# Row maxima of the next attention window: from five separate places of the loop to the two blocks of value products, with seven PSUM banks in one ring

## The chip, the cores and the metric

One core of one Trainium2 chip runs the whole kernel in one launch. The metric is the device time of one execution in microseconds; the figure for a kernel is the median of its runs. Views of the profile come from one further, profiled execution of the same program. The engines are called by the profile's short names: PE (TensorE, the matmuls), PEld (its weight loads), DVE (VectorE), ACT (ScalarE), POOL (GpSimd), SP (SyncE, which issues most DMAs).

## The reference, cut to what matters

The kernel computes one transformer layer with two mixers side by side: a convolution branch and a grouped-query attention branch fed by one input projection, merged by gates, then one output projection.

```python
# x (1, 1024, 1024), ctx (1, 256, 1024); 16 query heads of 64, 4 key/value heads
h  = rms_norm(x, g_pre) * (1 + sc) + sh          # hc the same from ctx
ua, gate_a, q, k, v, gate_b, gm = split_proj(h @ w_in)
q = apply_rope(rms_norm(q, q_norm_g));  k = apply_rope(rms_norm(k, k_norm_g))
k_all, v_all = latent and context keys, values    # 1280 keys
s = einsum('bqkgd,bskd->bkgqs', q, k_all) * HEAD_DIM**-0.5
p = softmax(s);  o = einsum('bkgqs,bskd->bqkgd', p, v_all)
y_attn = (o.reshape(b, n, 1024) * silu(gate_b)) @ w_attn_out
y_conv = conv_module(ua, gate_a, ...)             # 31 taps, layer norm, silu gates, matmul
mix = (sigmoid(ga) * y_conv + sigmoid(gb) * y_attn) @ w_out
out = x + gt * rms_norm(mix, g_post)
```

The softmax needs, for every query, a number close to its largest score, so that exp neither overflows nor vanishes. The kernel calculates these maxima in advance, with matmuls of their own.

## The kernel before, in words

All instructions are issued through the helper class `Ordered` (lines 41–54), so nearly every row of the profile carries line 51; one tells the work apart by the names of the tiles. A matmul's tile in PSUM is named after the tag of its bank with a p in front (`ps`, `ppj`, `po`).

**Before the attention loop** (to about 606 us of the span) the projections, the normalisations and the first taps of the convolution run. Projection work that is left over is kept in a generator, and `filler(n)` (1304) issues the next n of its steps, three matmuls of 128x512 each (`ppj<-t,whi` and `ppj<-t,wlo`, from `mm3`, 119, called in `proj`, 160).

**The attention loop** (1446) has 320 half-steps i, called steps here. A window w stands for a pair of heads e = 0, 1 and one half (512) of the queries; there are 16. Each goes through ten chunks c of 128 keys; `at = i % 20` is the step within a window. Per step it issues, in this order:

- `score` (919) for the next chunk: two matmuls `ps<-r,kk` into one bank, then on ACT the exponential `pe<-ps`, then sums of the exponentials (`psum` on POOL, `part` on DVE). Called S below.
- the pieces of the maxima, at some steps: `max_pieces` (867) for a later window. A piece has four tiles of one bank each, in two pairs; the matmuls of a pair use 64 rows of the array each, for e = 0 and 1 (`ps<-kk,rq`). On each tile DVE then does a TENSOR_REDUCE `mx<-ps`. Ten pairs m = 0…9 make a window. Called M below.
- at the end of a window's maxima `max_cols` (898), a small reduce `mc<-mx` on DVE; and at at=12 `max_rows` (903): a transpose `ps<-ident,mc` on PE, a negation `mr` on ACT, and two DMAs `r<-mr`, issued by ACT, that put the maxima in row 64 of the r2 operands of the next window's scores.
- at at=9 and at=19 (chunks 4 and 9) `weigh` (944): ten matmuls `po<-pe,vt`, of two 64-column halves side by side, that multiply five chunks of exponentials with the values; the profile records each as two, so 20. Called W.
- after the second W `pair_end` (961): eight small matmuls `ps<-psum,ones` (16 records) for the denominators, called D, two steps later `O<-gate,po` on DVE and the copy `og`, then the reciprocal, and ten steps after D `O<-O,R` on DVE.
- `filler(1)`: three projection matmuls, called F. So an ordinary step is S then F.

The engines work through their queues in the order in which the program issues. `urgent()` (116) keeps what is issued in it in the program's order; other work on DVE, ACT and POOL is placed by the scheduler of the framework between it. Beside the window's work DVE and POOL carry the rest of the convolution branch in the same stage (taps, `y<-y,acc`, layer norm, `ysum`, `z`) and the splitting of weights into two parts (`wlo`).

Where the maxima stand is set by two constants: `LEAD = 8` and `WINDOWS = (2, 7, 11, 14, 17)` (832–833). The loop takes `divmod(i + 8, 20)` and issues a piece where the remainder is in `WINDOWS`: at=14 and 19 for window w+2, at=3, 6 and 9 for window w+1. The pieces of at=9 and at=19 stand straight in front of a W; the other three stand between an S and an F. The queries for them are loaded by `max_load` (851), called at at=10 for window w+2.

PSUM has eight banks. In the loop `pj` has two (projections), `o` one (value products), and `s` five; scores, maxima, the transposed rows and the denominators all take the next of the five `s` in turn (`pt`, 90; `share`, 82; 1407–1408). Before the loop, at 1409–1423, the maxima of window 0 are issued as five pieces among filler steps, and the first two pieces of window 1 with `max_rows(0)` among four more.

## Time and profile before

| What | us |
|---|---|
| median of 3 runs (1410.0, 1413.3, 1412.09) | 1412.09 |
| profiled execution: its own time | 1411.38 |
| its span (first to last instruction) | 1409.6 |
| PE busy | 1351.9 (96% of the span) |
| DVE busy | 1043.1 (74%) |
| POOL busy | 687.6 (49%) |
| ACT busy | 564.7 (40%) |
| mean granted clock of PE | 0.989 |

The span is 1.8 us shorter than the profiled execution's own time, and that is 0.7 us under the median. In the profile "busy" of PE runs from a matmul's start to its modelled end, and successive matmuls overlap, so the time that a matmul takes in a stream is the distance to the next one's start, not its duration. A bracket at the end of a row of the timeline gives the engine's idle time before it and what ended that. Rows that stand directly behind one another with the same operation are shown as one row with a count.

### The profile page before, as it was taken

To read this page: it belongs to the slowest core of one execution; us is meant where nothing else is said; L and a number is where in the kernel's file an instruction comes from. 1 tells how busy PE (TensorE), PEld (TensorE's weight loads), DVE (VectorE), ACT (ScalarE), POOL (GpSimd) and SP (SyncE) were. 2 spreads that over 40 slices of the span, in tenths; PEclk is the share of its full clock that TensorE was granted. 3 is DMA by queue.
4 is the path that set the end of the run, shared out by engine and by line. 5 is a ranking of instruction groups with operands and counts; after the bars stand their busy time and mean duration, and the time that the engine had idled before them with its cause. 6 is when DMAs were issued, how large, how long until landed. Compare 5 with 4: busy or idle time off the path is not lost.

```text
span 1409.6 us, 19371 instructions
## 1 busy us (share of the span) xinstructions
PE 1351.9 (96%) x6520; PEld 1000.3 (71%) x6520; DVE 1043.1 (74%) x1359; ACT 564.7 (40%) x1388; POOL 687.6 (49%) x559
## 2 busy tenths in 40 slices
PE   5999999999999999999999999999999999999995
PEld 3768889887888877666666666666666565788774
DVE  3476988998889998885775566567676776349967
ACT  5542344343433332134444445445454434222333
POOL 1112257466556550054675556555556656263623
PEclk9999999999999999999999999999999999999998
DMA  9733434444444436523545444543365657699754
GB/s 317 272 127 105 137 109 159 140 167 150 136 144 134 152 111 185 163 90 116 177 152 171 135 120 147 183 144 120 113 197 173 214 194 263 218 315 347 242 186 154
DMA packets 153187, 242.41 MB, mean 172 GB/s; under 512 B 19792, under 2 KB 72572, under 8 KB 153088
## 3 DMA queue, kind: packets, MB, share of 16 engines
q1 hardware_dynamic: 139648, 218.03, 47.1%
q10 hardware_dynamic: 13440, 23.14, 5.6%
q8 instruction: 52, 0.85, 0.3%
q14 instruction: 47, 0.39, 0.1%
HBM read 161.46 MB, written 79.52 MB: 171 GB/s over the span
## 4 chain that ended last, share of the span: by engine, by line
PE 60%; DVE 16%; issue 7%; POOL 6%; DMA 5%; ACT 4%; SPq 1%; ACTq 1%; POOLq 0%; DVEq 0%
PE ppj L51 26%; PE ps L51 17%; PE po L51 14%; DVE pconv L51 7%; PE pm L51 3%; DVE t L51 2%; POOL wlo L51 2%; DVE qk L51 2%; DMA wm<-in_wmod 1%; DVE qkt L51 1%; POOL opw L51 1%; DVE acc L51 1%; ACT pe L51 1%; DVE r1st L51 1%; POOL y L51 1%
## 5 line engine op out<-in xcount | busy, mean ns | idle before, releaser
L51 PE MATMUL ppj<-t,whi 128*128 128x512 f32 x1728 | 621.0, 403 | 17.2 <-DVE y L51 9.1
L51 PEld LDWEIGHTS ppj<-t,whi 128*128 128x128 f32 x1728 | 327.8, 190 | 124.1 <-issue 36.5
L51 PE MATMUL ppj<-t,wlo 128*128 128x512 f32 x864 | 340.7, 394 | 0.0
L51 DVE TENSOR_REDUCE mx<-ps 128x1 f32<-128x512 f32 (+1 forms) x320 | 199.7, 682 | 109.8 <-PE ps L51 109.2
L51 ACT ACTIVATE pe<-ps 128x512 f32<-128x512 f32 x320 | 188.0, 597 | 191.8 <-PE ps L51 186.8
L51 DVE SCALAR_TENSOR_TENSOR pconv<-y,cw,pconv 128x1016 f32<-128x1016 f32 (+14 forms) x197 | 251.9, 1279 | 6.7 <-ACT pconv L51 2.0
L51 PE MATMUL ps<-r,kk 128*128 128x512 f32 (+1 forms) x640 | 199.9, 393 | 0.7 <-DMA r<-mr 0.7
L51 POOL TENSOR_TENSOR psum<-psum,pe 128x512 f32<-128x512 f32 x128 | 171.0, 1354 | 33.0 <-ACT pe L51 29.7
L51 PEld LDWEIGHTS ppj<-t,wlo 128*128 128x128 f32 x864 | 164.8, 191 | 29.3 <-issue 0.2
L51 PE MATMUL po<-pe,vt 128*64 128x512 f32 x640 | 144.4, 597 | 0.0
L51 PEld LDWEIGHTS ps<-r,kk 128*128 128x128 f32 (+1 forms) x640 | 120.3, 188 | 29.5 <-issue 0.8
L51 POOL TENSOR_TENSOR psum<-psum,part 128x512 f32<-128x512 f32 x64 | 90.6, 1417 | 100.7 <-DVE part L51 100.7
L51 POOL TENSOR_TENSOR wlo<-wraw,whi 128x512 fp32r<-128x512 f32 x59 | 79.8, 1361 | 118.7 <-ACT whi L51 117.1
L51 PE MATMUL po<-wgh,t 128*128 128x384 f32 x512 | 130.1, 335 | 0.0
L51 POOL TENSOR_TENSOR psum<-pe,pe 128x512 f32<-128x512 f32 x32 | 42.9, 1359 | 122.5 <-ACT pe L51 122.5
L51 PEld LDWEIGHTS po<-pe,vt 128*64 128x64 f32 x640 | 43.1, 136 | 81.0 <-issue 78.9
L51 PEld LDWEIGHTS po<-wgh,t 128*128 128x128 f32 x512 | 92.7, 188 | 1.4 <-ACT qk L51 0.2
L51 PE MATMUL po<-wgl,t 128*128 128x384 f32 x256 | 85.8, 335 | 0.3 <-DVE wgl L51 0.3
L51 ACT CAST whi<-wraw 128x512 fp32r<-128x512 f32 x112 | 68.7, 634 | 42.0 <-PE ppj L51 22.4
L51 DVE TENSOR_TENSOR part<-pe,pe 128x512 f32<-128x512 f32 x64 | 66.2, 1038 | 19.4 <-ACT pe L51 19.3
L51 DVE TENSOR_TENSOR wlo<-wraw,whi 128x512 fp32r<-128x512 f32 x53 | 45.7, 865 | 45.5 <-ACT whi L51 45.4
L51 PE MATMUL ps<-kk,rq 64*128 64x512 f32 (+1 forms) x384 | 67.9, 405 | 4.9 <-ACT pe L51 3.1
(211 smaller groups left out, 1776.9 us busy)
## 6 DMA issues: line engine op xcount, KB each, us to landing
wraw<-in_wch SPq DMA_DIRECT2D x96, 256.0 KB
opD<-opw SPq DMA_DIRECT2D x56, 256.0 KB
wm<-in_wmod SPq DMA_DIRECT2D x24, 512.0 KB
W<-opD SPq DMA_DIRECT2D x48, 256.0 KB
r1D<-r1st SPq DMA_DIRECT2D x32, 256.0 KB
y<-accD SPq DMA_DIRECT2D x16, 512.0 KB
r<-r1D ACTq DMA_DIRECT2D x32, 256.0 KB
opD<-acc SPq DMA_DIRECT2D x13, 512.0 KB
```

The lines of the kernel that those rows point to most:

```text
L51: i = f(*a, **k)
```

## The change

The constants `LEAD` and `WINDOWS` give way to `AROUND = (((0, 1, 2), (3, 4)), ((5, 6, 7), (8, 9)))`, and `max_pieces` takes a tuple of pairs. At each W the first tuple is issued in front of it and the second behind it: at at=19 the pairs 0–4 of window w+2, at at=9 the pairs 5–9 of window w+1, followed by `max_cols`. No pairs are issued anywhere else in the loop. Pairs 4 and 9 have four matmuls of 256 in place of two of 512; they stand behind. At at=19 the first part of `pair_end` (D) is now issued straight after W, ahead of the pairs behind it; in the code before it came after W and ahead of F as well. `max_load` moves from at=10 to at=6, and `max_rows` (still at at=12) is issued ahead of the maxima in the code.

The two `pj` and five `s` banks become seven tags of one bank each: p0, p1, b0…b4. `pt` hands out the tag that was handed out or let go longest ago, and not one in `busy`: the bank of the projection in progress is held until its result is evacuated, that of D until its copy `og` is issued. From step 2·NS − 24 on (`ending`) projections take only p0 and p1. Before the loop the row `max_rows(0)` comes after two filler steps, and window 1 gets its first five pairs (three, then two filler steps, then two, then two); the loop is entered after 26 filler steps in place of 24 from the first maxima on, so two fewer are left for the time behind the loop.

```diff
-    def pt(tag, shape=(P, 512), dtype=F32):
-        if not any(tag in bufs for _, _, bufs in shares):
-            tag = "s"
+    def pt(tag, shape=(P, 512), dtype=F32, hold=None):
+        if tag == "pj" or len(turns) > 2 and tag in ("s", "m"):
+            to = turns if tag != "pj" or not ending else [t for t in turns if t[0] == "p"]
+            tag = next(t for t in to if len(turns) == 2 or t not in busy.values())
+            turns.remove(tag)
+            turns.append(tag)
+            if hold is not None:
+                busy[hold] = tag
...
+    def let_go(what):
+        tag = busy.pop(what)
+        turns.remove(tag)
+        turns.append(tag)
...
-    LEAD = 8
-    WINDOWS = (2, 7, 11, 14, 17)
+    AROUND = (((0, 1, 2), (3, 4)), ((5, 6, 7), (8, 9)))
...
-    share({"s": 5})
+    share({f"b{i}": 1 for i in range(5)})
+    turns[:0] = [f"b{i}" for i in range(5)]
...
-    for i in range(LEAD):
-        if i in WINDOWS:
-            max_pieces(1, WINDOWS.index(i))
-        if i % 2:
-            filler(1)
-        if i == 3:
-            max_rows(0)
+    filler(2)
+    max_rows(0)
+    for ms in AROUND[0]:
+        max_pieces(1, ms)
+        filler(2)
...
-        if at == 18 - LEAD and w + 2 < NW:
+        if at == 6 and w + 2 < NW:
             max_load(w + 2)
...
+        if i == 2 * NS - 24:
+            ending.append(True)
         if n + 1 < NS:
             score(n + 1, e)
-        ahead, piece = divmod(i + LEAD, 2 * NKC)
-        if ahead + 1 < NW and piece in WINDOWS:
-            max_pieces(ahead + 1, WINDOWS.index(piece))
-            if piece == WINDOWS[-1]:
-                max_cols(ahead + 1)
-        if at == 20 - LEAD and w + 1 < NW:
+        if at == 12 and w + 1 < NW:
             max_rows(w + 1)
         if e and c % BATCH == BATCH - 1:
+            ahead, around = (w + 2, AROUND[0]) if c == NKC - 1 else (w + 1, AROUND[1])
+            if ahead < NW:
+                max_pieces(ahead, around[0])
             weigh(n)
-        if e and c == NKC - 1:
-            later(i, pair_end(w))
+            if c == NKC - 1:
+                g = pair_end(w)
+                later(i + next(g), g)
+            if ahead < NW:
+                max_pieces(ahead, around[1])
+                if c < NKC - 1:
+                    max_cols(ahead)
```

**PE, in the tenth window (w = 9).** Before, a piece stands by itself between a score (`r1`, `r2`) and a filler step: here the third of the five for window 10 (its queries are `rq_2097`), at at=6.

```order
L51 MATMUL ps_2172_9288<-r1_2030_8781,kk_1841_8118 128x512
L51 MATMUL ps_2172_9288<-r2_2031_8782,kk_1842_8119 128x512
L51 MATMUL ps_2175_9296<-kk_1841_8118,rq_2097_9024 128x512
L51 MATMUL ps_2176_9297<-kk_1841_8118,rq_2097_9024 128x512
L51 MATMUL ps_2177_9300<-kk_1841_8118,rq_2097_9024 128x512
L51 MATMUL ps_2178_9301<-kk_1841_8118,rq_2097_9024 128x512
L51 MATMUL ppj_2169_9276<-t2_25_126,whi_2103_9049 128x512
```

In the changed kernel nothing stands there but score and filler, and the pairs 5, 6 and 7 of window 10 (`rq_2071`) stand between the score at at=9 and the first value product. The sixth tile takes p1, the bank of the score directly ahead; the other five take banks whose scores and maxima are older.

```order
L51 MATMUL pp1_2185_9336<-r1_2030_8785,kk_1846_8137 128x512
L51 MATMUL pp1_2185_9336<-r2_2031_8786,kk_1847_8138 128x512
L51 MATMUL pb3_2187_9342<-kk_1846_8137,rq_2071_8934 128x512
L51 MATMUL pp0_2188_9343<-kk_1846_8137,rq_2071_8934 128x512
L51 MATMUL pb1_2189_9346<-kk_1846_8137,rq_2071_8934 128x512
L51 MATMUL pb2_2190_9347<-kk_1846_8137,rq_2071_8934 128x512
L51 MATMUL pb0_2191_9350<-kk_1846_8137,rq_2071_8934 128x512
L51 MATMUL pp1_2192_9351<-kk_1846_8137,rq_2071_8934 128x512
L51 MATMUL po_2193_9360<-pe_2131_9145,vt_1848_8142 64x512
```

Behind the last value product of the same block stand the pairs 8 and 9, in the first four banks of the six again, and then the filler step.

```order
L51 MATMUL po_2193_9360<-pe_2178_9313,vt_1848_8142 64x512
L51 MATMUL pb3_2194_9371<-kk_1846_8137,rq_2071_8934 128x512
L51 MATMUL pp0_2195_9372<-kk_1846_8137,rq_2071_8934 128x512
L51 MATMUL pb1_2196_9375<-kk_1846_8137,rq_2071_8934 128x256
L51 MATMUL pb2_2197_9376<-kk_1846_8137,rq_2071_8934 128x256
L51 MATMUL pb1_2196_9375<-kk_1846_8137,rq_2071_8934 128x256
L51 MATMUL pb2_2197_9376<-kk_1846_8137,rq_2071_8934 128x256
L51 MATMUL pb4_2161_9251<-t2_35_136,whi_2109_9074 128x512
```

**DVE, ahead of the small reduce `mc` of the sixth window (w = 5).** Before, the last four reduces on tiles, `O<-O,R` of the window before, and then `mc`:

```order
L51 TENSOR_REDUCE mx_1712_7649<-ps_1789_7914 128x1
L51 TENSOR_REDUCE mx_1712_7649<-ps_1790_7915 128x1
L51 TENSOR_REDUCE mx_1712_7649<-ps_1791_7918 128x2
L51 TENSOR_REDUCE mx_1712_7649<-ps_1792_7919 128x2
L51 TENSOR_TENSOR O_1749_7782<-O_1749_7782,R_1765_7835 128x512
L51 TENSOR_REDUCE mc_1793_7928<-mx_1712_7649 128x8
L51 TENSOR_TENSOR y4_1699_7601<-y4_1699_7601,acc_1666_7481 128x512
```

In the changed kernel a sum of the convolution branch has come ahead of `mc` as well, and the four reduces belong to the pairs behind W (the six of the pairs in front stand ahead of these rows).

```order
L51 TENSOR_REDUCE mx_1733_7722<-pb2_1793_7938 128x1
L51 TENSOR_REDUCE mx_1733_7722<-pp0_1794_7939 128x1
L51 TENSOR_REDUCE mx_1733_7722<-pb1_1795_7942 128x2
L51 TENSOR_REDUCE mx_1733_7722<-pb0_1796_7943 128x2
L51 TENSOR_TENSOR O_1751_7796<-O_1751_7796,R_1766_7840 128x512
L51 TENSOR_TENSOR y4_1701_7611<-y4_1701_7611,acc_1664_7481 128x512
L51 TENSOR_REDUCE mc_1797_7952<-mx_1733_7722 128x8
```

The transpose that reads `mc` stands on PE at at=12 as before, three steps behind this block. In the changed kernel only `O<-O,R` stands between the last tile's reduce and `mc` in nine windows (as in all fourteen of the kernel before that have an `O`), and one further instruction of the convolution branch in the windows 5, 6, 8, 9 and 12.

**DVE, at the entry of the loop.** Before, the last reduces of window 0 are followed by one of window 1, by `mc`, and by seven more of window 1:

```order
L51 TENSOR_REDUCE mx_1190_5771<-ps_1219_5899 128x2
L51 TENSOR_REDUCE mx_1190_5771<-ps_1220_5900 128x2
L51 TENSOR_REDUCE mx_1222_5914<-ps_1223_5915 128x1
L51 TENSOR_REDUCE mc_1221_5909<-mx_1190_5771 128x8
L51 TENSOR_REDUCE mx_1222_5914<-ps_1224_5916 128x1
```

In the changed kernel a tap of the convolution (`acc<-y,cw,acc`) stands on either side of `mc`, and the third front tile of window 1 (`pb3_1227`) is the last of the six to be reduced:

```order
L51 TENSOR_REDUCE mx_1190_5771<-pb2_1220_5900 128x2
L51 SCALAR_TENSOR_TENSOR acc_1133_5425<-y4_1079_5079,cw_85,acc_1133_5425 128x1015
L51 TENSOR_REDUCE mc_1221_5909<-mx_1190_5771 128x8
L51 SCALAR_TENSOR_TENSOR acc_1133_5425<-y4_1079_5079,cw_85,acc_1133_5425 128x1014
L51 TENSOR_REDUCE mx_1224_5923<-pb0_1225_5924 128x1
L51 TENSOR_REDUCE mx_1224_5923<-pp1_1226_5925 128x1
L51 TENSOR_REDUCE mx_1224_5923<-pb1_1228_5929 128x1
L51 TENSOR_REDUCE mx_1224_5923<-pb4_1230_5933 128x1
L51 TENSOR_REDUCE mx_1224_5923<-pb2_1229_5932 128x1
L51 TENSOR_REDUCE mx_1224_5923<-pb3_1227_5928 128x1
```

On POOL the sums of the exponentials and those of the convolution branch (`y`) change places at one spot that matters: before the denominators of window 14 three `y` additions stand directly ahead of the two last `psum<-psum,part` in the kernel before (one more stands a row earlier), and in the changed kernel one, with the other three behind the two sums.

More of the change, by code (lines that the diff above doesn't have):

```diff
@@ L88, in unshare @@
             shares.pop()[0].__exit__(None, None, None)
-    def pt(tag, shape=(P, 512), dtype=F32):
-        if not any(tag in bufs for _, _, bufs in shares):
-            tag = "s"
+    turns = ["p0", "p1"]
+    busy = {}
+    ending = []
+    def pt(tag, shape=(P, 512), dtype=F32, hold=None):
[6 more added lines that the diff above has]
+                busy[hold] = tag
         for _, pool, bufs in shares:
@@ L95, in pt @@
                 return pool.tile(list(shape), dtype, tag=tag, bufs=bufs[tag], name=nm("p" + tag))
-    share({"pj": 2})
+    def let_go(what):
+        tag = busy.pop(what)
+        turns.remove(tag)
+        turns.append(tag)
+    share({"p0": 1, "p1": 1})
     share({"m": 2, "o": 2})
@@ L162, in proj @@
         his, los = w
-        p = pt(tag)
+        p = pt(tag, hold="pj")
         for k in range(KD):
@@ L169, in proj @@
                     evac(p, slice(hf * 512, hf * 512 + 512))
+                let_go("pj")
             yield
@@ L865, in block_kernel, with max_pieces @@
     mxs = {}
-    def max_pieces(w, n):
-        if n == 0:
+    def max_pieces(w, ms):
+        if ms[0] == 0:
             mxs[w] = tl("mx", (P, 2, 4, 3), 2, pool="B")
@@ L874, in max_pieces @@
         todo = []
-        for m in (2 * n, 2 * n + 1):
+        for m in ms:
             i, j = divmod(m, 5)
@@ L962, in pair_end @@
         pr, tok = w // 2, halfq(w)
-        p = pt("m", (P, 2, P))
+        p = pt("m", (P, 2, P), hold=w)
         for e in range(2):
@@ L972, in pair_end @@
         S.copy(dn[:], p[:])
+        let_go(w)
         dc = tl("dc", (P, 8), 2, pool="B")
@@ L1407, in block_kernel @@
     share({"o": 1})
-    share({"s": 5})
+    share({f"b{i}": 1 for i in range(5)})
+    turns[:0] = [f"b{i}" for i in range(5)]
     for i in range(5):
         filler(4)
-        max_pieces(0, i)
+        max_pieces(0, (2 * i, 2 * i + 1))
         with tc.issue_after(crit[0].ins):
@@ L1484, in block_kernel @@
     unshare(2)
+    turns[:] = [t for t in turns if t[0] == "p"]
     share({"m": 2, "o": 2})
```

## The prediction

> **What bounds the kernel now.** I read the page first, then the stretch of one window, then what PE waits for in the loop. On the page PE is busy for nearly all of the span. The stretch (columns: start and end, length, then busy time with the number of records for PE, PEld, DVE, ACT and POOL, granted clock, DMA share, GB/s) is an ordinary window. The last view gives engine, tile waited for, total, times and the longest, for 606 to 1220 us.
>
> ```profile
> PE 1351.9 (96%) x6520; PEld 1000.3 (71%) x6520; DVE 1043.1 (74%) x1359; ACT 564.7 (40%) x1388; POOL 687.6 (49%) x559
> ```
>
> ```profile
> 906.00:943.30 37.30, 37.30 (x184) 23.52 (x183) 22.28 (x36) 17.15 (x29) 21.75 (x15) 1.00 0.53 169
> ```
>
> ```profile
> PE ps L51 <- ACT pe L51: 3.1, 4, 1.5
> PE ps L51 <- POOL psum L51: 2.6, 2, 1.4
> PE ps L51 <- DMA r<-mr: 0.7, 2, 0.4
> PE ps L51 <- DVE mx L51: 0.5, 1, 0.5
> ```
>
> PE has no idle time in this window; in the whole loop these waits, all that the view has, make 6.9 us. DVE is busy 22.28 of 37.30 us, so it has room on average. A change is thus worth what it alters in the spacing of the matmuls, and it loses what it adds in waits of PE. The PE timeline of a stand-alone block gives the spacing (start, duration, engine, line, operation, tile, records):
>
> ```profile
> 919.68 0.62 PE L51 MATMUL ps<-r,kk 128*128 128x512 f32 x2
> 920.22 0.73 PE L51 MATMUL ps<-kk,rq 64*128 64x512 f32 x4
> 920.89 0.50 PE L51 MATMUL ppj<-t,whi 128*128 128x512 f32 x1
> 921.22 0.40 PE L51 MATMUL ppj<-t,wlo 128*128 128x512 f32 x1
> 921.46 0.39 PE L51 MATMUL ppj<-t,whi 128*128 128x512 f32 x1
> 921.69 0.63 PE L51 MATMUL ps<-r,kk 128*128 128x512 f32 x2
> ```
>
> In the stream a matmul takes 0.23 us to the next start (921.22 to 921.46 to 921.69), so a score of two takes 0.46. With M behind it the score takes 0.54 to 0.55, some 0.09 more; M with two pairs takes 0.67 (0.66 below); the first F behind M takes 0.33 (920.89 to 921.22), 0.10 more. So a stand-alone block costs 0.66 + 0.09 + 0.10 = 0.85. The next rows are the block at at=19 of the same window, M in front of W:
>
> ```profile
> 924.01 0.62 PE L51 MATMUL ps<-r,kk 128*128 128x512 f32 x2
> 924.56 0.73 PE L51 MATMUL ps<-kk,rq 64*128 64x512 f32 x6
> 925.22 4.51 PE L51 MATMUL po<-pe,vt 128*64 128x512 f32 x20
> 929.66 0.50 PE L51 MATMUL ppj<-t,whi 128*128 128x512 f32 x1
> ```
>
> Here M costs 0.66 alone, since W needs the slow score ahead and the slow F behind (0.50 long) in any case.
>
> **The maxima, before.** The loop has 73 blocks: 44 stand alone, 29 in front of a W. That is 44 × 0.85 + 29 × 0.66 = 56.5 us. To it come the late blocks. The longest is this, where three matmuls go and the fourth waits for a bank, because an exponential is late:
>
> ```profile
> 1124.10 0.77 PE L51 MATMUL ps<-kk,rq 64*128 64x512 f32 x3
> 1126.37 0.67 PE L51 MATMUL ps<-kk,rq 64*128 64x512 f32 x1 [1.49 <-ACT pe L51]
> 1126.97 0.80 PE L51 MATMUL ppj<-t,whi 128*128 128x512 f32 x1
> ```
>
> ```profile
> 935.74 0.97 PE L51 MATMUL ps<-kk,rq 64*128 64x512 f32 x4
> 936.64 0.50 PE L51 MATMUL ppj<-t,whi 128*128 128x512 f32 x1
> ```
>
> The first is 2.87 − 0.66 = 2.2 late; the second, 0.90 − 0.66 = 0.24, is an ordinary one. There are 21 late blocks, between these two rows in kind, and they add up to 11.1. So the maxima cost PE 56.5 + 11.1 = 67.6, say 68 us.
>
> **The maxima, after.** There are 29 blocks in front and 29 behind. In front a third pair adds two stream halves, about one 0.23 step: 0.66 + 0.23 = 0.89. But the sixth tile takes the bank of the score directly ahead and must wait for its exponential. When that comes, and how long a lone last matmul takes, these rows show:
>
> ```profile
> 924.02 0.62 ACT L51 CAST whi<-wraw 128x512 fp32r<-128x512 f32 x1
> 924.72 0.60 ACT L51 ACTIVATE pe<-ps 128x512 f32<-128x512 f32 x1
> ```
>
> ```profile
> 1087.33 0.50 PE L51 MATMUL ps<-kk,rq 64*128 64x512 f32 x1 [1.02 <-ACT pe L51]
> 1087.76 0.50 PE L51 MATMUL ppj<-t,whi 128*128 128x512 f32 x1
> ```
>
> The exponential starts 0.71 after its score (924.01 to 924.72) and, 0.60 long, ends at 1.31; if the signal takes 0.05 (an assumption of mine) the sixth matmul starts 1.36 after the score, and W 0.43 later (1087.33 to 1087.76), at 1.79. M began at 0.55, so the block takes 1.24, 0.35 of it wait. Behind W two pairs take 0.66; the slow F behind them was paid by W already. That is 29 × (1.24 + 0.66) = 55.1 us, 12.9 less than 68, if nothing else is late. Two things can be.
>
> *Late exponentials.* At at=19 casts like the one at 924.02 stand between the exponentials; one that is issued late holds the score's exponential by up to 0.62. Over 14 such blocks the ends are 0 and 8.7; most casts find ACT idle, as that one does, so I take **+3**, with 0 to 8.
>
> *The small reduce `mc`.* It must come before the transpose at at=12. From the end of W, PE gets there after M (0.66), F (0.79), two steps of 1.16 and a score (0.46): 4.23 us. On DVE the four reduces start 0.53 after M's start and take 0.60 each (598.53, 599.06 and the x5 row below), so `O<-O,R` starts at 2.93. What it then takes:
>
> ```profile
> 924.36 1.77 DVE L51 TENSOR_TENSOR y<-y,acc 128x512 f32<-128x512 f32 x1
> 926.06 2.47 DVE L51 TENSOR_REDUCE mx<-ps 128x1 f32<-128x512 f32 x4
> 928.45 0.71 DVE L51 TENSOR_TENSOR O<-O,R 128x512 f32<-128x512 f32 x1
> 929.08 0.16 DVE L51 TENSOR_REDUCE mc<-mx 128x8 f32<-128x24 f32 x1
> ```
>
> ```profile
> 924.28 1.31 POOL L51 TENSOR_TENSOR psum<-psum,pe 128x512 f32<-128x512 f32 x1 [0.80 <-ACT pe L51]
> ```
>
> ```profile
> L51 DVE TENSOR_TENSOR O<-O,R 128x512 f32<-128x512 f32 x16 | 17.7, 1104 | 2.3 <-DMA R<-recD 2.3
> ```
>
> Alone such an addition takes 0.71; beside a POOL addition, as at 924.36, it took 1.77; the mean of the sixteen `O<-O,R` is 1.10. With 0.16 for `mc` PE waits from nothing (0.71: ready at 3.80) to 0.65 (1.77: ready at 4.88). POOL's next `psum` becomes ready at about the time that `O<-O,R` starts, so either can win. In the five windows with a further instruction between, it is 0.3 to 2.1. That gives bounds of 0 and 9 × 0.65 + 5 × 2.1 ≈ 17; with the group's mean 1.10 the nine windows wait about nothing to 0.2, the five about 1.3: I take **+8**. So the maxima cost 55.1 + 3 + 8 = 66.1: **−1.9**.
>
> **Entry of the loop.**
>
> ```profile
> 598.53 0.73 PE L51 MATMUL ps<-kk,rq 64*128 64x512 f32 x6
> ```
>
> ```profile
> 583.21 1.27 DVE L51 SCALAR_TENSOR_TENSOR acc<-y,cw,acc 128x1018 f32<-128x1018 f32 x1
> ```
>
> ```profile
> 599.06 3.08 DVE L51 TENSOR_REDUCE mx<-ps 128x1 f32<-128x512 f32 x5
> ```
>
> After the last block of window 0 (598.53) PE now has only two filler steps, 0.66 + 1.48, and reaches the transpose at 600.67; the four reduces end at 601.46 and the tap ahead of `mc` takes 1.2, so the transpose goes at about 602.85: 2.2 lost. The second tap ends at 604.1, six reduces last to 607.7, and the block behind, which PE reaches at about 605.2 for its first pair, needs the bank that is reduced last: 2.0 to 2.5 lost. About 0.3 to 0.5 is won, waits for `r<-mr` that the later scores no longer have. Sum **+3.9**, with 0 (if the scheduler's taps were covered) to 6. The two filler steps that move here from the tail are the same work in both places.
>
> **The denominators of window 14.** PE waited for POOL's last sums, behind three `y` additions:
>
> ```profile
> 1177.42 0.43 PE L51 MATMUL ps<-psum,ones 128*32 128x128 f32 x8 [1.38 <-POOL psum L51]
> 1179.09 0.43 PE L51 MATMUL ps<-psum,ones 128*32 128x128 f32 x8 [1.24 <-POOL psum L51]
> ```
>
> ```profile
> 1170.62 3.40 POOL L51 TENSOR_TENSOR y<-y,y 128x512 f32<-128x512 f32 x2
> ...
> 1175.67 3.37 POOL L51 TENSOR_TENSOR psum<-psum,part 128x512 f32<-128x512 f32 x2
> ```
>
> With one `y` ahead in place of three the sums start over 3 us earlier, and 1.38 + 1.24 go: **−2.6** (0 if `y` is late too).
>
> **The clock.** The columns are as above, of PE alone.
>
> ```profile
> 586.80:590.80 4.00, 4.00 (x12) 0.57 0.00 0
> 1126.30:1130.00 3.70, 3.63 (x8) 0.54 0.22 87
> ```
>
> In these two stretches of about 4 us the mean granted clock is 0.57 and 0.54, so it was at about half for some 3.4 us; the second is the gap of 1.49 at 1126.37 and what follows. Half of 3.4 us is 1.7 lost, and the gap at 1126 stood in a stand-alone block that is gone: **−1.7** (+1.7 if a new gap of that size brings a dip). The gap of 1.02 at 1087.33 had none: the matmuls behind it last 0.50, as at 920.89. By the Trainium skill ("TensorE: Matmul & The Clock Gate", section "Why this matters for your kernels") only idle gaps over some 3 us throw the clock back. By that rule the dip is no consequence of the gap, this term is nothing and the sum 1.7 higher; the trace has a dip directly behind a gap of 1.49 and so disagrees, on one instance.
>
> **The rest.** `max_load` four steps earlier puts two DMA issues of ACT three steps ahead of a block in place of directly behind one; ACT uses 0.60 of each step's 1.16 for its exponential and catches up between: nothing, and what it doesn't catch up lies in the 0 to 8 of the late exponentials. D directly behind W is where it was: nothing. Projections and scores now share seven banks; a bank comes round after seven tiles, several steps, and its exponential ends 1.31 after its score: nothing, or a share of those 0 to 8. The ones that do come round sooner are the sixth tile (costed) and, at the entry, the bank reduced last (costed). Two filler steps (0.70 each) fewer in the tail leave up to 1.4 uncovered there: **+0.5**.
>
> **Sum.** −1.9 + 3.9 − 2.6 − 1.7 + 0.5 = −1.8: the profiled execution at 1411.38 − 1.8 = 1409.6, and 0.7 more on the scale of the median: 1410.3. One can tell from no change what is over 0.2%, 2.8 us. My forecast is thus no change, 1410.3, with 1407 to 1415 if only the small terms miss. Chance 0.32.
>
> **Rival A, faster.** The saved spacing is kept: POOL loses the races, `mc` costs 1 in all, no exponential is late. For it speaks the share of DVE (22.28 of 37.30). Then −12.9 + 1 + 3.9 − 2.6 − 1.7 + 0.5 = −11.8: 1400.3. Chance 0.39, counting all that falls below 1409.3.
>
> **Rival B, slower: evacuation becomes the bound.** Ten tiles come in one block, DVE needs ten times 0.60 for them, and PE comes to the transpose of `mc` and to the sixth tile before they are ready. At the upper ends (17 and 8): −12.9 + 25 + 3.9 − 2.6 − 1.7 + 0.5 = +12.2: 1424.3. It decides from 4.6 us over my 8 on, that is when the transposes wait 0.84 on average over fifteen windows. For it stands that eleven reduces and `O<-O,R` now fall into some 7 us, against it that in the window above DVE is idle for 15. Chance 0.29. The skill's page "TensorEngine Tiling (Array Packing)", section "PSUM Bottleneck", warns of this: splitting the array speeds up TensorE and not the evacuation of PSUM. The trace of before does not bear it out: PE waited 0.5 us in all for `mx`.
>
> **Rival C: the stand-alone place was not what cost.** If the matmuls behind W pay a change of mode of their own, 0.10 on either side, M costs 5.8 more: 1416; it lies within B's chance.
>
> **Range.** 1399 takes in A, 1423 nearly all of B; 2 in 10 lie outside. Faster by over 0.2% has 0.39, same 0.32, slower 0.29.
>
> **What would show it.** A block in front takes 1.24 with a gap before its last matmul put down to `pe`; the transposes at at=12 show waits for `mc` of 0 to 0.7, in the windows 5, 6, 8, 9, 12 more; no halved clock near 1126; no wait for `psum` in window 14; first F of the loop some 5 us later (3.9 and the 1.4 of two filler steps). I am wrong if the transposes' waits add up to under 3 or over 13, if the front blocks take 0.89 or over 1.6, or if new waits of PE for banks of projections appear.

## The result, and the profile after

The changed kernel takes 1437.72 us (median of five runs, 1436.87 to 1439.3), the kernel before beside it 1413.3 (five runs, 1410.0 to 1416.24). The ratio is 1.0176, with a 95% interval of 1.0158 to 1.0195: slower by 24 us, outside the stated range of 1399 to 1423. The profiled execution has a span of 1435.9 us against 1409.6. Most of the 26.3 us between the spans arose inside the loop: from the start of the first W to that of the last it took 586.7 us before and 613.7 after, +27.0. The way up to the first W is 1.8 longer and the tail behind the last W 2.5 shorter.

The page's line of busy times, and what PE waited for in the loop (606 to 1250 us):

```profile
PE 1362.4 (95%) x6520; PEld 1012.8 (71%) x6520; DVE 1101.5 (77%) x1359; ACT 559.4 (39%) x1388; POOL 718.6 (50%) x559
```

```profile
PE pb L51 <- DVE mc L51: 6.6, 6, 2.3
PE pb L51 <- ACT pe L51: 6.0, 8, 1.4
PE pp L51 <- ACT pe L51: 5.5, 4, 2.8
PE pp L51 <- DVE mc L51: 2.2, 3, 1.0
PE pb L51 <- DVE mx L51: 0.8, 1, 0.8
PE pb L51 <- DVE ts L51: 0.2, 1, 0.2
```

The waits made 6.9 us before and 21.3 now. The more telling number is DVE's: the same 1359 instructions keep it busy 58 us longer. (A PE wait in this view is idle time to the modelled end of the matmul before; by starts the losses are larger.)

A punctual block looks as forecast. PE around the W of chunk 4 in window 6:

```profile
859.38 0.62 PE L51 MATMUL pb<-r,kk 128*128 128x512 f32 x2
859.93 0.73 PE L51 MATMUL pb<-kk,rq 64*128 64x512 f32 x3
860.27 0.39 PE L51 MATMUL pp<-kk,rq 64*128 64x512 f32 x1
860.50 0.69 PE L51 MATMUL pb<-kk,rq 64*128 64x512 f32 x2
861.12 4.51 PE L51 MATMUL po<-pe,vt 128*64 128x512 f32 x20
865.56 0.62 PE L51 MATMUL pb<-kk,rq 64*128 64x512 f32 x3
...
866.22 0.50 PE L51 MATMUL pp<-t,whi 128*128 128x512 f32 x1
...
871.01 0.27 PE L51 MATMUL pb<-ident,mc 128*8 128x128 f32 x1 [1.04 <-DVE mc L51]
```

The front block takes 1.19 (859.93 to 861.12), the block behind 0.66 (865.56 to 866.22). The median of the 29 front blocks is 1.24 and that of the 29 behind 0.67. The last row is a transpose that came 1.2 us late. DVE and POOL in the same stretch show why:

```profile
860.58 2.47 DVE L51 TENSOR_REDUCE mx<-pb 128x1 f32<-128x512 f32 x4
862.97 0.68 DVE L51 TENSOR_REDUCE mx<-pp 128x1 f32<-128x512 f32 x1
863.57 0.68 DVE L51 TENSOR_REDUCE mx<-pb 128x1 f32<-128x512 f32 x1
866.09 1.89 DVE L51 TENSOR_REDUCE mx<-pb 128x1 f32<-128x512 f32 x3 [1.85 <-PE pb L51]
867.90 0.68 DVE L51 TENSOR_REDUCE mx<-pp 128x2 f32<-128x512 f32 x1
868.50 0.68 DVE L51 TENSOR_TENSOR O<-O,R 128x512 f32<-128x512 f32 x1
869.09 1.77 DVE L51 SCALAR_TENSOR_TENSOR y<-ysum,y 128x512 f32<-128x512 f32 x1
870.79 0.17 DVE L51 TENSOR_REDUCE mc<-mx 128x8 f32<-128x24 f32 x1
```

```profile
862.98 2.50 POOL L51 TENSOR_TENSOR psum<-psum,pe 128x512 f32<-128x512 f32 x2
868.49 5.21 POOL L51 TENSOR_TENSOR psum<-psum,pe 128x512 f32<-128x512 f32 x3 [3.02 <-ACT pe L51]
```

While W runs no exponentials come, so POOL has nothing to add from 865.5 to 868.5. In that gap DVE is at the reduces. As soon as DVE comes to its additions, POOL adds without a break, and the addition that should take 0.70 takes 1.77.

The whole loop shows the same. Over its 31 half-windows, from one W's start to the next, each cut into fourteen equal parts (1.35 us before, 1.41 after), the busy shares in percent are, counted from all records of the two traces:

```
part of the half-window    1   2   3   4   5   6   7   8   9  10  11  12  13  14
before  POOL              81  63  47  27  28  74  99  97  91  52  30  24  73  68
        DVE, reduces      70  81  28   7   0   0   0  24  85  62  23  27  52  10
        DVE, other        21  19  46  65  35  28  17  15   4  39  39  20  12  20
after   POOL              81  67  39  19  11  39  92  98  90  88  75  55  63  73
        DVE, reduces      81  99  43  37  89  67   7   2   0   0   0   0   0  32
        DVE, other        11   5  11   5   9  44  91  75  67  47  33  26  27  20
```

("Other" leaves out the sums `part`.) Before, DVE's additions lay in the parts 3 to 5, where POOL was idle more than half of the time. After, the reduces lie there, and the additions are in the parts 7 to 10, where POOL is busy nine tenths. Of the two-input additions of DVE in the loop 137 were free of POOL before and 93 were not, 0.70 and 1.34 us each; after, 48 and 179, 0.68 and 1.35. (Free means that POOL worked in less than three tenths of the addition; with no overlap at all it is 110 of 230 before and 45 of 227 after.) The reduces don't care: 0.68 beside POOL and without it, in both kernels. POOL's own sums take 1.30 alone, 1.50 (before) and 1.61 (after) beside DVE. The largest group of the convolution branch, of before and then of after, in the groups by line:

```profile
L51 DVE TENSOR_TENSOR y<-y,acc 128x512 f32<-128x512 f32 x32 | 29.6, 940 | 0.0
```

```profile
L51 DVE TENSOR_TENSOR y<-y,acc 128x512 f32<-128x512 f32 x32 | 51.0, 1621 | 0.0
```

From DVE the delay goes through ACT to PE. The block in front of W at at=19 of window 1, in the order DVE, POOL, ACT, PE:

```profile
669.79 0.17 DVE L51 TENSOR_REDUCE mc<-mx 128x8 f32<-128x24 f32 x1
669.88 7.89 DVE L51 TENSOR_TENSOR y<-y,acc 128x512 f32<-128x512 f32 x4
```

```profile
669.19 5.23 POOL L51 TENSOR_TENSOR psum<-psum,pe 128x512 f32<-128x512 f32 x3 [4.66 <-ACT pe L51]
674.49 2.73 POOL L51 TENSOR_TENSOR ysum<-ysum,y 128x1024 f32<-128x1024 f32 x1
```

```profile
677.85 1.06 ACT L51 ACTIVATE y<-y 128x1024 f32<-128x1024 f32 x1 [1.39 <-DVE y L51]
678.82 0.58 ACT L51 ACTIVATE pe<-pb 128x512 f32<-128x512 f32 x1
...
680.73 1.16 ACT L51 CAST whi<-wraw 128x512 fp32r<-128x512 f32 x2
681.75 0.63 ACT L51 ACTIVATE pe<-pp 128x512 f32<-128x512 f32 x1
```

```profile
678.26 0.62 PE L51 MATMUL pp<-r,kk 128*128 128x512 f32 x2
678.81 2.10 PE L51 MATMUL pb<-kk,rq 64*128 64x512 f32 x4
680.91 0.49 PE L51 MATMUL pp<-kk,rq 64*128 64x512 f32 x1
682.43 0.50 PE L51 MATMUL pp<-kk,rq 64*128 64x512 f32 x1 [1.03 <-ACT pe L51]
682.86 1.51 PE L51 MATMUL po<-pe,vt 128*64 128x512 f32 x6
```

Four additions of 0.7 take 7.89 us beside POOL. ACT's next operation of the branch waits for them, and the exponentials stand behind it in ACT's queue; the one of the score at 678.26 runs at 681.75 in place of 678.97. The sixth tile needs its bank. The block takes 4.05 (678.81 to 682.86) in place of 1.24. Two casts of weights, the kind that the prediction had in mind, stand in that queue too and hold the exponential by another 1.0 (680.73 to 681.75).

Not every late block is of this kind. Ten front blocks take over 1.6 us, together 17.2 over 1.24 each. By ACT's rows eight of them, with 15.1 of the 17.2, stand behind an operation on ACT that waited for sums of the branch: four for DVE's (5.6) and four for POOL's (9.5). Two (2.1) stand behind casts that waited for a DMA.

The clock, of PE alone as in the prediction: two of the seven stretches at half clock in the loop (the kernel before has one), and a stretch behind the gap of 1.04 at 871.01 that is not slowed.

```profile
988.00:991.60 3.60, 3.60 (x10) 0.54 0.37 147
1114.60:1118.20 3.60, 3.50 (x9) 0.53 0.92 262
871.00:874.60 3.60, 3.59 (x17) 1.00 0.34 139
```

### The profile page after: what moved, and what is told of

It reads as the page before. It is cut to its first block, busy times and chain, and to the rows that moved or that the text cites. A ratio compares the mean times of both kernels' runs of the same rounds, so it can differ in the third digit from the quotient of the medians.

```text
span 1435.9 us, 19346 instructions
## 1 busy us (share of the span) xinstructions
PE 1362.4 (95%) x6520; PEld 1012.8 (71%) x6520; DVE 1101.5 (77%) x1359; ACT 559.4 (39%) x1388; POOL 718.6 (50%) x559
## 5 line engine op out<-in xcount | busy, mean ns | idle before, releaser
L51 PE MATMUL pp<-t,whi 128*128 128x512 f32 x1200 | 408.0, 401 | 19.6 <-DVE y L51 7.8
L51 PEld LDWEIGHTS pp<-t,whi 128*128 128x128 f32 x1200 | 228.8, 191 | 78.3 <-issue 8.0
L51 PE MATMUL pp<-t,wlo 128*128 128x512 f32 x600 | 237.2, 395 | 0.0
L51 PE MATMUL pb<-t,whi 128*128 128x512 f32 x528 | 211.7, 405 | 0.0
L51 ACT ACTIVATE pe<-pb 128x512 f32<-128x512 f32 x226 | 133.1, 598 | 114.1 <-PE pb L51 99.3
L51 DVE TENSOR_REDUCE mx<-pb 128x1 f32<-128x512 f32 (+1 forms) x225 | 143.7, 681 | 37.8 <-PE pb L51 19.9
L51 PE MATMUL pb<-r,kk 128*128 128x512 f32 x452 | 142.0, 396 | 0.0
L51 PEld LDWEIGHTS pp<-t,wlo 128*128 128x128 f32 x600 | 114.9, 192 | 21.6
L51 PEld LDWEIGHTS pb<-t,whi 128*128 128x128 f32 x528 | 100.0, 189 | 26.2 <-issue 1.3
L51 PE MATMUL pb<-t,wlo 128*128 128x512 f32 x264 | 104.6, 396 | 0.0
```

Of the source, the lines that this page charges most:

```text
L51: i = f(*a, **k)
```

## The experiments

The theories, by the letters of the expectations. At first: A, the convolution branch's work on DVE, POOL and ACT delays `mc` and the exponentials; B, PE's waits stand for one another; C, the shared ring of banks is the loss; D, ten tiles at one place are too much for DVE by themselves. After the first series: S, the sixth front tile has no slack. When S had fallen I counted DVE's additions by whether POOL was adding, made the table above, and formed P: the reduces take POOL's idle time away from the additions.

Each run is compared with the kernel before, run on the same chip in the same series; before's median was 1412.3, 1413.3 and 1412.0 in the three series. The part ahead of the loop differs by several us between executions: the first W starts at 619.8 us in the kernel before and at 614.0 in the kernel that differs from it only inside the loop. So I give the loop's length (first W to last W) as well; it is that of the one profiled execution of each kernel. Where nothing else is said, an edit is one of the changed kernel.

**The two halves of the change.** First the ring of seven banks with the maxima at their old places. Against the kernel before (`pt`, `turns`, `busy`, `let_go` and `ending` as in the changed kernel, the rest as before):

```diff
-    share({"s": 5})
+    share({f"b{i}": 1 for i in range(5)})
+    turns[:0] = [f"b{i}" for i in range(5)]
...
```

> The kernel before with the seven banks handed out in one ring and nothing else changed: the maxima stand at their five places as before. Theory A (the places are the cause of the loss): 1406 to 1414, since the late blocks of before (11.1 us) have more banks to choose from and nothing else is altered. Theory C (projections that share banks with scores wait for exponentials; in the changed kernel three or four filler matmuls waited 3.6 us for a bank): slower than before, 1418 or more, with waits of PE for pe ahead of filler matmuls.

Measured: 1405.46 us, ratio 0.9949 (0.9923 to 0.9976), loop 580.6. What PE waits for:

```profile
PE pb L51 <- POOL psum L51: 2.3, 2, 1.2
PE pb L51 <- DVE ts L51: 1.4, 1, 1.4
PE pb L51 <- DVE mx L51: 0.7, 2, 0.4
PE pb L51 <- ACT pe L51: 0.6, 1, 0.6
```

The ring alone is a gain of 7 us, and this is the fastest of the kernels that leave nothing out: it beats both. The 73 blocks of maxima take 51.3 us in all, 3.2 over their punctual 0.66 each, where before they were 11.1 over. Of these 11.1 us 8.0 stood at one place: all fourteen blocks at at=14, two steps behind the transpose, were late. ACT issues the row's two DMAs ahead of them, and the exponentials that stand behind the issues come late, as in front of the block at 935.74:

```profile
934.20 1.31 ACTq L51 DMA_DIRECT2D r<-mr  x2
935.56 1.08 ACT L51 ACTIVATE pe<-ps 128x512 f32<-128x512 f32 x2 [1.39 <-PE ps L51]
```

(Issuing isn't counted as busy, so the view puts the gap down to PE; the first of the two scores had started at 934.04.) With the ring the same fourteen blocks are 0.2 late in all. Theory C falls. DVE's additions stay where they were (136 free of POOL, 94 not).

Then the places of the change with the banks of before:

```diff
-    share({f"b{i}": 1 for i in range(5)})
+    share({"s": 5})
 pt, proj, pair_end as before; AROUND and all else as in the changed kernel
```

> The changed kernel's places with the banks of before (two for projections, five in turn for scores, maxima and the rest): the other half of the change by itself. In front the fifth tile now takes the bank of the score directly ahead and the sixth that of the first tile, which its reduce must free. The first reduce ends 1.2 us after the block's start, about when the score's exponential does, so theory S expects the punctual block at 1.6 to 1.7 in place of 1.24 (29 blocks: +10 to +14), the late ones as late as in the changed kernel, and no filler matmul waiting for a bank (3.6 less): 1441 to 1452. If the ring itself were the loss (theory C) this run would be at 1412 to 1425.

Measured: 1473.71, ratio 1.0437 (1.0396 to 1.0479), loop 643.7.

```profile
PE ps L51 <- DVE mx L51: 19.6, 16, 3.7
```

Worse than expected: the punctual front block is 1.70 as worked out, but 13 of 28 are above 1.9, up to 6.8. In these 13 PE waits 14.1 us for reduces and 9.9 for exponentials, and nine stretches at half clock, 51 us in all, come on top. So the places cost some 32 us with the ring (1405.5 to 1437.7) and 60 without (1413.3 to 1473.7), and the ring gains in either. The loss is in the places.

**Are PE's waits for `mc` the loss?**

```diff
-        if at == 12 and w + 1 < NW:
+        if at == 14 and w + 1 < NW:
             max_rows(w + 1)
```

> The changed kernel with one edit: the transpose of the maxima, and with it the row's two DMAs, two steps later (at=14 in place of at=12). Its profile showed nine of the fifteen transposes late, 10.2 us in all, 8.6 + 2.2 of it put down to mc. Theory A (each wait of PE is its own loss): the transposes are on time, 10 us go, and one or two of the eight stretches at half clock (1.7 each) with them: 1424 to 1428. Theory B (the transposes only take a loss early that the blocks at at=19 would have had anyway, since the exponentials there are late through other work): the waits for mc go, the blocks in front of W get longer, and the time stays at 1434 to 1439. Either way the maxima's row must reach the next window's first score in four steps (4.6 us) in place of six; if it doesn't, a new wait for the row's DMA shows.

Measured: 1432.83, ratio 1.0140 (1.0112 to 1.0168), loop 603.6. The waits for `mc` are gone, and 7.0 us of waits for the row's DMA have come (six, up to 3.0). Half of the 10 us are left as a gain, in the range of neither theory: part of the loss came back as other waits.

The next run moves the transpose one step only and takes `O<-O,R` from between:

```diff
-        if at == 12 and w + 1 < NW:
+        if at == 13 and w + 1 < NW:
...
-        yield 5
+        yield 7
         V.tensor_tensor(out=O[:], in0=O[:], in1=R[:], op=ALU.mult)
```

> The changed kernel (three pairs in front, two behind) with the same two edits alone: transpose at at=13, O<-O,R two steps later. The waits for mc (10.2 us) go, without the row's DMA coming late as it did at at=14. Theory S: the front blocks stay late (12 to 17 us over 1.24 each), so 1422 to 1430. Theory D: hardly anything is gained, 1432 or more.

Measured: 1438.41, ratio 1.0193 (1.0158 to 1.0229), loop 609.4. No wait for `mc` is left, and nothing is gained:

```profile
PE pb L51 <- ACT pe L51: 7.8, 11, 2.2
PE pp L51 <- ACT pe L51: 6.1, 4, 4.1
PE pp L51 <- DMA r<-mr: 2.9, 1, 2.9
```

The waits for exponentials rose from 11.5 to 13.9 us, the front blocks from 52.4 to 55.8, and the wait of one filler matmul for a bank from 2.84 to 4.13. The waits of PE that went came back at the next places where PE needs DVE or ACT. So theory B is right on this, and a sum of PE's waits, as in the prediction, prices nothing here.

**Is it the sixth tile that has no slack?**

```diff
-    AROUND = (((0, 1, 2), (3, 4)), ((5, 6, 7), (8, 9)))
+    AROUND = (((0, 1), (2, 3, 4)), ((5, 6), (7, 8, 9)))
```

> The changed kernel with two pairs in front of each W and three behind, so pairs 0, 1 and 5, 6 in front. No front tile takes the bank of the score directly ahead any more: the last one takes that of the score two steps earlier, 2.3 us more slack for a late exponential. In the changed kernel the blocks in front took 52.4 us for 29, 16.4 over the 1.24 each that a punctual exponential gives. Theory S (what costs most is that the sixth tile has no slack, so every late exponential on ACT passes to PE in full): blocks in front 0.66 with under 4 us of lateness in all, behind 0.89, together 45 + 4. The transposes at at=12 come worse off, as six reduces in place of four stand ahead of mc: 1.2 each, 10 us become 18 to 25. Sum: 1418 to 1428. Theory D (DVE can't do ten tiles in a window's half): the lateness moves behind W and to the transposes in full, 1434 to 1445.

Measured: 1438.23, ratio 1.0190 (1.0155 to 1.0226), loop 609.0. The front blocks take 27.3 us, 8.2 over their 0.66 each; so 2.3 us more of slack only halves the lateness. The waits for `mc` grew from 8.8 to 15.5 in the view (17.6 by starts; 18 to 25 were expected). One thing I had overlooked: at at=19 the denominators and the projection hold a bank each, five are left, and the sixth tile behind W waits 0.8 for the first one's reduce, fourteen times. The next run has this edit, the transpose at at=13 and `O<-O,R` two steps later together:

> As the run with two pairs in front and three behind, and also the transpose one step later (at=13) and O<-O,R two steps later, so that it no longer stands between the reduces and mc. Theory S: waits for mc fall to 2 to 8 us, waits for the row's DMA stay under 2, late blocks as in that run: 1398 to 1410, that is under the kernel before. Theory D: 1420 or more, with the waits on mx banks or in the later steps.

Measured: 1426.07, ratio 1.0100 (1.0066 to 1.0135), loop 598.4. Both lie where theory D had put them, and theory S falls as the main cause. It holds in one place: in the last third of the loop (the last eleven half-windows) these two kernels take 207.3 and 211.4 us, the changed kernel 218.6, the kernel before 206.8.

**Is it the convolution branch?** Its variance and normalisation are left out of both kernels:

```diff
         ln_mean()
-        yield 6
-        yield from ln_var()
-        yield from z_prep()
+        ln["z"] = True
```

> The changed kernel without the variance and the normalisation of the convolution branch (the generators that spread them over the loop are left out, so DVE, ACT and POOL do nothing of this branch in the windows 1 to 11; the splits of its result in the last windows stay). Theory A (the loss comes from this branch: its additions on DVE run beside POOL's sums, are late, and hold mc on DVE and the exponentials behind them on ACT): up to window 11 all blocks in front of W take 1.24 and no transpose waits; the time is 20 to 30 us under the changed kernel, 1408 to 1418, and 8 to 13 under the kernel before with the same left out. Theory D (ten tiles at one place are too much for DVE by themselves): the waits for mc and the long blocks stay, the time is within 10 us of the changed kernel's and over that of the kernel before with the same left out.

> The kernel before without the same work of the convolution branch, as the other end of the pair. PE was short of work for 7 us in its loop, and 21 blocks of maxima were late by 11.1 us in all. Theories A and D alike: the late blocks go up to window 11, so 4 to 9 us under the kernel before, 1404 to 1409. By theory A the changed kernel with the same left out is 8 to 13 us below this one; by theory D above it.

Measured: 1418.84 (ratio 1.0038, 1.0020 to 1.0056) for the changed kernel and 1402.97 (0.9929, 0.9905 to 0.9953) for the one before. By its totals theory A is wrong: the changed kernel stays 16 us behind. By stage it is half right. The first twenty half-windows, in which the branch has now no work, take 370.9 us in the changed kernel and 374.9 in the one before; every front block there takes 1.18 to 1.25, no transpose waits, and PE waits once, where it waited 9.9 us in the complete kernel (both in the stretch 606 to 1020):

```profile
PE pb L51 <- DVE mx L51: 0.6, 1, 0.6
```

So the move gains 4.0 us there with nothing against it, 3.1 of them from the late blocks at at=14, which the kernel before has with and without the branch. ACT's casts of weights are still issued among the exponentials in this part, so casts alone make no block late. The last eleven, in which ACT's casts of the next stage still wait for sums on POOL, take 228.0 against 207.4 (in the complete kernels 218.6 against 206.8). So the branch's work on DVE, POOL and ACT beside the maxima is needed for the loss, and what remained of it in the last windows is enough for 20 us.

**Is it POOL beside DVE?** POOL's running sums are left out of both (and the reciprocal replaced), the convolution branch is whole:

```diff
-        elif c not in (0, 3, 8):
-            G.tensor_tensor(out=acc_p[w, e][:], in0=acc_p[w, e][:], in1=x[:], op=ALU.add)
         if c in (4, 9):
-            G.tensor_tensor(out=acc_p[w, e][:], in0=acc_p[w, e][:], in1=part.pop((w, e))[:], op=ALU.add)
+            part.pop((w, e))
...
-        V.reciprocal(rc[:], dc[:])
+        V.tensor_scalar(out=rc[:], in0=dc[:], scalar1=1.0, scalar2=1.0, op0=ALU.mult, op1=ALU.add)
```

> The changed kernel without POOL's running sums of the exponentials (all but the first addition of each window and head is left out, and the reciprocal of the denominators is replaced by a harmless operation of the same size). What it is for: in the loop DVE's two-input additions take 0.70 us when POOL is idle and 1.35 when POOL adds at the same time. In the kernel before 137 of 230 were free of POOL, in the changed one 48 of 227, and DVE's busy time rose by 40 us for the same work. Theory P (the ten reduces at a W take the time in which POOL has nothing to add; the convolution branch's additions are pushed to where POOL adds without a break, last twice as long, and ACT and with it the exponentials wait behind them): without POOL's sums the additions take 0.7 wherever they stand, the late blocks and most waits for mc go, and this kernel is no more than 4 us over the kernel before with the same left out, or below it: 1396 to 1410. Theory D (ten tiles at one place are too much for DVE whatever POOL does): 12 us or more above that kernel, 1418 or more.

> The kernel before with the same sums and the reciprocal left out, the other end of the pair. The waits for psum (2.6 us) go, some of the 11.1 us of late blocks too: 1401 to 1410 by either theory. Theory P: the changed kernel with the same left out stands at most 4 us above; theory D: 12 or more above.

Measured: 1405.19 (ratio 0.9946, 0.9927 to 0.9966) and 1397.89 (0.9903, 0.9869 to 0.9936). In the changed kernel now 172 additions are free of POOL and 55 not, the transposes are late by 0.7 in all (10.2 with POOL's sums), and of PE's waits this is left:

```profile
PE pb L51 <- ACT pe L51: 2.7, 3, 1.9
PE pb L51 <- DVE mx L51: 0.6, 1, 0.6
PE pp L51 <- ACT pe L51: 0.5, 1, 0.5
```

The loops are 580.6 and 578.3 us: the change costs 2.3 in the loop where it cost 27.0 with POOL's sums. In the first twenty half-windows it gains 3.8 (with POOL's sums it lost 15.3), in the last eleven it loses 6.1 (11.8). Most of these 6.1 is one front block, at 1036.09, which takes 4.29 behind casts that wait for a DMA, with 6.8 us at half clock in it and behind it. The whole times are 7.3 apart, more than the 4 of theory P and less than the 12 of theory D; the profiled executions reach the first W 5.8 us apart. The kernel before gained more than the 1401 to 1410 expected of it. All ten tiles still stand at the two Ws, DVE still does their reduces in one go. So theory D falls: the burst of reduces by itself costs little, and it costs because of what it pushes into POOL's busy time. Since the edit also frees POOL's queue for the branch's own sums, it doesn't separate the slower additions from POOL's later ones.

**Two smaller steps.** The spread work ahead of the maxima in each step:

```diff
+        for g in late.pop(i, []):
+            with tc.issue_after(crit[0].ins), urgent():
+                d = next(g, None)
+            if d is not None:
+                later(i + d, g)
         if e and c % BATCH == BATCH - 1:
             ahead, around = (w + 2, AROUND[0]) if c == NKC - 1 else (w + 1, AROUND[1])
...
-        for g in late.pop(i, []):
-            with tc.issue_after(crit[0].ins), urgent():
-                d = next(g, None)
-            if d is not None:
-                later(i + d, g)
```

> The changed kernel with one thing moved: at each step the spread work (the convolution branch's next operation, the later parts of a window's end) is issued ahead of the pairs of maxima in front of W, not behind those behind it. So what is due at the two W steps of a window runs on DVE ahead of the six reduces, in the time in which POOL has nothing to add. Theory P: of the 86 additions that lost their POOL-free time only those due at these two of twenty steps come back, some 10 to 30, so 1425 to 1435, with fewer late blocks in the first eight windows. Theory D: the reduces come later by 0.7, the blocks behind W and mc with them: 1436 to 1445.

Measured: 1437.81, ratio 1.0175 (1.0139 to 1.0212), loop 611.3. No addition came back: 41 free of POOL, 186 not. The expectation of theory P fails here, in its guess that the work due at the W steps matters. The waits for `mc` fell to 2.6 and waits for `mx` rose to 9.8, once more a loss that moved.

Half way, on the kernel with the ring alone, the piece of at=6 behind the W at at=9:

```diff
-        if ahead + 1 < NW and piece in WINDOWS:
-            max_pieces(ahead + 1, WINDOWS.index(piece))
-            if piece == WINDOWS[-1]:
-                max_cols(ahead + 1)
+        if ahead + 1 < NW and piece in WINDOWS and piece != WINDOWS[3]:
+            max_pieces(ahead + 1, min(WINDOWS.index(piece), 3))
...
             weigh(n)
+            if ahead + 1 < NW and piece == WINDOWS[4]:
+                max_pieces(ahead + 1, 4)
+                max_cols(ahead + 1)
```

> Half way: the ring of seven banks, the places of before, but the piece of at=6 put behind the W at at=9 (with the piece of two pairs that stood in front of it unmoved), so one stand-alone block fewer per window: 15 x 0.19 = 2.9 us less of matmul spacing. Eight reduces stand at one W of each window, four at the other. Theory P: the additions of DVE that fall beside POOL's rise from 94 to 110 to 140, for up to 0.65 us each of DVE time but with DVE free 30% of the loop, and mc comes late in some windows: 1402 to 1412, between the ring alone (1405.5) and a small loss. Theory D: the burst counts by its size, 8 in place of 10: 1412 to 1425.

Measured: 1411.21, ratio 0.9994 (0.9975 to 1.0013), loop 586.1, 5.5 over the ring alone in spite of 2.9 us less spacing; 122 additions beside POOL. That is the upper end of theory P's range. Among the kernels with the ring and the whole work the time rises with that count, roughly: 94 (ring alone, 1405.5), 122 (this, 1411.2), 172 (two in front and three behind, 1426.1 with both edits and 1438.2 without), 179 to 186 (the changed kernel and three others, 1432.8 to 1438.4). Among the last six the count doesn't order the times.

## Why the prediction was wrong, point by point

The sum for the loop, as predicted and as the trace of after has it:

| Term | predicted | measured |
|---|---|---|
| blocks if punctual, 55.1, against 67.6 before | −12.9 | −12.5 |
| late blocks ("late exponentials") | +3 | +18.5 |
| transposes waiting for `mc` | +8 | +10.2 |
| half clock | −1.7 | +10.2 |
| denominators of window 14 | −2.6 | −2.6 |
| a filler matmul waiting for a bank | 0 | +3.0 |
| sum | −6.2 | +26.8 (the loop: +27.0) |

- *Spacing.* Right but for a rounding, 67.6 to 68, that gave the change 0.4 too much: 1.24 in front with 0.35 of wait in it, 0.66 behind. Yet only 1.4 of the 12.5 (56.5 against 55.1) is spacing; the other 11.1 are late blocks of the kernel before, and 8.0 of these went with the ring alone, without moving anything. The front blocks add up to 52.4 us, 16.4 over 29 × 1.24; those behind to 21.2, 2.1 over 29 × 0.66.
- *Late exponentials: this is the step that failed.* I put them down to casts, bounded them at 8.7 and took 3, "most casts find ACT idle, as that one does". Most of the lateness came from elsewhere: operations of the convolution branch on ACT wait for DVE's or POOL's additions, and hold the exponentials behind them (15.1 us in front, as counted above); casts alone make no block late (the run without the branch). I had the row for it, 1.77 beside POOL against 0.71, and used it for `O<-O,R` alone, whose mean hardly moved (1.13 to 1.12 in the loop). For all other additions I kept before's durations, as if moving the reduces left them in place. I never asked which work stood in POOL's idle time during W. The runs with the branch or with POOL's sums left out show that it is this.
- *Transposes.* Nine were late by 10.2 in all, inside 0 to 17 (the bound's terms add up to 16.4) and near the 8: the five windows with a further instruction by 1.2 to 2.4, as forecast, and four others by 0.7, close to the 0.65 forecast for an `O<-O,R` beside POOL. But without these waits (the run with the transpose at at=13) the time is the same, so their price was right and their meaning wrong.
- *Clock.* The second large miss. I counted one dip (a stretch at half clock) gone. The gap at 1126 is gone, but seven dips came, six more than before, 1.7 each. Five of them start within 2.4 us behind gaps of 1.3 to 2.8 us of PE; the other two (742.6 and 769.9) have no gap over 0.6 us in the six us ahead of them, and their cause stays open. The parenthesis "+1.7 if a new gap of that size brings a dip" named the mechanism for one gap. The rule of the Trainium skill ("TensorE: Matmul & The Clock Gate", section "Why this matters for your kernels"), that only gaps over some 3 us do it, is not what this trace shows: none of the five gaps is over 2.84.
- *Entry.* The number is near, in part by luck. From the last block of window 0 to the first score it took 6.2 us before and 11.1 after, less 1.4 for two filler steps: +3.5; to the first F of the loop, behind before's wait for `r<-mr`, +2.9. Predicted was +3.9. The transpose there waited for `mc` as predicted (2.2):

```profile
601.71 0.27 PE L51 MATMUL pb<-ident,mc 128*8 128x128 f32 x1 [2.01 <-DVE mc L51]
```

  But the 2.0 to 2.5 for the bank reduced last did not come: the block behind takes 1.17 (605.79 to 606.96), 0.5 over a punctual one. In its place the clock fell to half from 602.6 to 606.0, 1.7 lost, which the sum did not have.

- *Tail.* −2.5 us, of which 1.4 are the two filler steps; the rest, −1.1, against +0.5.
- *"Projections and scores now share seven banks ... nothing."* A filler matmul waited 2.84 us for a bank (1210.13; 3.0 by starts), behind an exponential that ACT ran late; a new wait of this kind was one of the signs of being wrong. By itself the ring is a gain of 7 us, which I gave no value.
- *Rival B* had the direction, not the mechanism, and its upper end, 1424.3, is 13 us under the measured 1437.7: it decides, I wrote, where the transposes wait 0.84 on average; they waited 0.68, and the loss came through ACT and the clock. Its counter-argument, DVE idle for 15 of 37 us, is the average that the table by part of the half-window takes apart. The warning of the Trainium skill quoted there ("TensorEngine Tiling (Array Packing)", section "PSUM Bottleneck"), that the evacuation of PSUM may become the bound, isn't what decided here: the reduces were as fast as before (0.68), and PE waited 0.8 us for `mx` in the loop. With the banks of before PE did wait for the reduces, 19.6 us.
- *Rival C* is out: the medians of both kinds of block are the punctual ones. *Rival A*, which trusted DVE's share of 22.28 us in 37.30, is out with the same average.

Not settled: how much of the loss is DVE's slower additions and how much POOL's own later sums, since both go when POOL's sums are left out. Of the 15.1 us of late front blocks counted above 9.5 stand behind POOL's sums of the branch and 5.6 behind DVE's; the waits for `mc` are DVE's.

## What to carry to other kernels

Before you gather an engine's work into one place, look at what it does there now and why there: most of DVE's additions stood where POOL was idle, and the place that looked free on PE was the one that DVE and POOL needed. Make a table of busy shares by part of the period, per engine; a mean over the window hides this. When PE's waits have several causes, a sum of them prices nothing unless an experiment shows that a removed wait stays away.

## What the runs showed of the hardware

- A two-input addition of DVE on 128x512 f32 takes 0.70 us alone and 1.34 on average beside an addition of POOL, 1.97 on average in the row of four shown; POOL's takes 1.30 alone and 1.50 to 1.61 beside DVE's. A reduce of DVE out of PSUM takes 0.68 in both cases. The Trainium skill has the rule, without these times ("SBUF — State Buffer", section "Who interferes with whom"): an instruction of DVE with two SBUF inputs contends with one of GpSimd that reads SBUF; one with at most one SBUF input, outside the modes that use two ports, doesn't. The traces agree, and this is what the prediction should have weighed against the change.
- The granted clock halves for 3.4 us, 1.7 of them lost (in some runs for 6.8), behind far shorter gaps of PE than the Trainium skill ("TensorE: Matmul & The Clock Gate", section "Why this matters for your kernels") lets one expect with its 3 us. In the loops of these kernels no lone gap of 0.9 to 1.1 us was followed by a dip; of 1.2 to 1.9 some were (1126.37 of before) and some weren't (1177.42); of the five of 2.2 to 2.3 in the run with two pairs in front and three behind three were; and all ten gaps from 2.27 to 4.3 were. Gaps are not the only cause: the dip at 760.7 of the run with the ring alone has none over 0.3 us in the six us ahead of it. The late transpose at 987.02, with 2.27 us of idle time and a dip behind it, cost about 4.
- Two DMA issues held ACT's queue for 1.31 us (934.20 of before). The view of waits puts the gap of 1.39 behind them down to PE, as issuing isn't counted as busy.
